# A decoder layer in one kernel: half-pace solve, merged columns turned outside TensorE, and the output projection's first steps

## The chip, the cores and the metric

The kernel runs on one core of one Trainium2 chip. The metric is the device time of one execution in microseconds. In the texts PE is TensorE (with PEld its weight loads), DVE is VectorE, ACT is ScalarE, POOL is GpSimd and SP is SyncE, whose queue issues nearly all transfers here.

## The reference

One decoder layer on 256 tokens of width 2048, all in fp32. The parts that bear on the change:

```python
def rms_norm(x, w):
    xf = x.astype(jnp.float32)
    y = xf * lax.rsqrt(jnp.mean(xf * xf, axis=-1, keepdims=True) + NORM_EPS)
    return (y * w.astype(jnp.float32)).astype(x.dtype)

# in chunk_gated_delta_rule, per head and chunk
t_mat = lax.linalg.triangular_solve(eye + a_mat, jnp.broadcast_to(eye, a_mat.shape),
                                    left_side=True, lower=True, unit_diagonal=True)
u = jnp.einsum('bhncs,bhnsv->bhncv', t_mat, v * beta[..., None])
...
```

The layer computes h = rms_norm(x) and projects it. Two branches follow, a gated delta rule of 8 heads (branch A, which holds the triangular solve above) and block-sparse attention of 8 heads (branch B). Each branch is taken to width 2048 by a matrix of its own, both are multiplied by sigmoid gates that are projected from h, and they are added ("merged"). An output projection of the merged values is added to x. A second norm and a gated MLP of width 5632, with a convolution of width 3, end the layer, and a last norm gives the output.

## The kernel before

Every product of width is done as three products of fp32r halves: a weight chunk of 128x2048 is fetched by SP into one of four buffers `wraw` (`fetch`, L121), cast by ACT in two pieces to `wh` (L111), and DVE writes the rest `wl` = raw - `wh` (L108). `wh` and `wl` have two buffers each, so ACT can cast a chunk only when PE has finished the chunk before the last. One chunk gives PE 24 matmuls with 512 moving columns, or as many columns in pairs of 512 and 256.

The work beside the weights runs as generators in the list `bg`. `main_mm` (L100 to 105) adds up the columns of the weight matmuls and calls `tick` after every 8 matmuls of 512 columns, and a tick advances each generator to its next `yield`. All engines take their instructions in program order, so the ticks set where this work stands between the weight matmuls on PE, the casts on ACT and the `wl` subtractions on DVE.

The stages around the change, in order:

- **Branch A's solve** (`gdn_unit`, L534 to 654) is done twice, for heads 0 to 3 (unit 0) and 4 to 7 (unit 1). The 32x32 diagonal blocks are inverted by 31 steps of two DVE instructions each (L561 to 567), a transfer to DRAM and back (tiles `dT` and `TL`, L568 and L570) puts them in place, and after 12 ticks DVE transposes 32x32 blocks (L574, tile `U`). Two levels of small matmuls with PE, DVE and POOL in turn, then `u`, `r`, `u`, `po` follow, each a tick apart. After `po`, POOL squares (L635), DVE reduces (L637), ACT takes a root, DVE scales (L644, tile `ot`), and four ticks later PE transposes 8 blocks (`pot`, L652). Unit 1 runs beside the gate projections:

```python
            if r % (2 - u["n"]) == 0:
                yield
```

so unit 0 does two steps a tick and unit 1 one.

- **Gates** (L756 to 769): 8 groups of 512 columns, `by_token`, in tiles `gts`. Before the sigmoids of group 4, unit 1 must have ended:

```python
        if c == 4:
            while ("end", 1) not in done:
                tick()
```

- **Branch projections** (L800 to 810): for each group c of 512 columns, 2 chunks of `w_ba` and 2 of `w_bb`, PSUM tiles `ps_br` with tokens on partitions. DVE multiplies by the gates and adds (L804 to 809). `merged(c, i)` (L789 to 798) then has PE transpose four 128x128 blocks of the 128 tokens i (`pt_m`, L794), ACT copies the result to `mc` and DVE writes the low half. `mc` has channels on partitions.
- **Output projection** (L819 to 843): 8 column groups `ps_wo` of two chunks each. The PSUM pools are opened anew (L812). The first group starts before the last merged group is there, by `steps`, and L160 lets the remaining ticks run before the step `flush`.
- **rstd** (L214 to 221) sums squares over the partitions by fp32 matmuls with a matrix of ones: two for the first norm (R1), four for the second (R2).
- **Down projection** (L875 to 911): the eight PSUM banks are taken in a fixed order.

Of the kernel before, what the change touches and what calls it, by code (L numbers as in the profile page):

```python
# [11 lines left out]
F32 = mybir.dt.float32  # L12
# [3 lines left out]
ALU = mybir.AluOpType  # L16
AX = mybir.AxisListType
PSUM = bass.MemoryType.PSUM

P = 128  # L20
# [53 lines left out]
def layer_kernel(ctx: ExitStack, tc: tile.TileContext, xT, pos, cst, ceye, vec, convw, ffw, bdv,  # L74
# [72 lines left out]
    def psum_pools(mm, sd):  # L147
        if pst[2]:
            pst[2].close()
        pst[2] = ExitStack()  # L150
        pst[0] = pst[2].enter_context(tc.tile_pool(name="ps_mm", bufs=mm, space=PSUM, reuse_waits="tile"))
        pst[1] = pst[2].enter_context(tc.tile_pool(name="ps_sd", bufs=sd, space=PSUM, reuse_waits="tile"))

    psum_pools(3, 5)

# [59 lines left out]
    def rstd(parts, tp, name):  # L215
        ps = sdt(name)[:, :T]
        mmg(ps, [(ones, t) for t in parts])
        r = tp.tile([P, T], F32, name=name)
        act.activation(r, ps, AF.Sqrt, bias=epst, scale=1.0 / D)
        dve.reciprocal(r, r)  # L220
        return r
# [67 lines left out]
        dve.tensor_tensor(sq[2], sq[2], sq[3], op=ALU.add)  # L289
    dve.tensor_tensor(sq[0], sq[0], sq[2], op=ALU.add)  # L290
    dve.tensor_tensor(sq[0][:, 0:2], sq[0][:, 0:2], sq[0][:, 2:4], op=ALU.add)


    wb2 = g.tile([P, KD, 48], F32R, name="wb2")
# [2 lines left out]
    low(wb2[:, :, 0:16], wb2[:, :, 32:48], wbd)  # L297
    s = sdt("ps_bd")[:48, :T]
    mmg(s, [(wb2[:, k, :], x_[:, k, :]) for k in range(KD) for x_ in (hh, hl)])
    R1 = rstd([sq[0][:, 0, :], sq[0][:, 1, :]], fk, "R1")  # L300
    R1b = both(R1)
    beta = fk.tile([16, T], F32, name="beta")
    sint = fk.tile([48, T], F32, name="sint")
# [235 lines left out]
    def gdn_unit(u):  # L539
# [21 lines left out]
        for r in range(30, -1, -1):  # L561
            tm = gu.tile([P, 8, 32], F32, name="tm", tag="Tm", bufs=1)
            n = 32 - r
            dve.tensor_tensor(tm[:, :, :n], X[:, :, r:], N[:, r:r + 1, r:].to_broadcast([P, 8, n]), op=ALU.mult)
            dve.tensor_reduce(X[:, :, r], tm[:, :, :n], axis=AX.X, op=ALU.add, negate=True)
            if r % (2 - u["n"]) == 0:
                yield
        pool.dma_start(bass.AP(tensor=dT.tensor, offset=dT.offset, ap=[[32 * P + 32, 32], [8 * P, 4], [P, 8], [1, 32]]), X)  # L568
        TL = gu.tile([P, 8, P], F32, name="TL", tag="u", bufs=1)
# [86 lines left out]
    def pair(w, i):  # L656
        return [w[2 * i], w[2 * i + 1]]
# [128 lines left out]
    m = m_st.enter_context(tc.tile_pool(name="mp", bufs=1, reuse_waits="tile"))  # L786
    mc = m.tile([P, KD * 2 * T + 128], F32R, name="mc")[:, SHIFT:SHIFT + KD * 2 * T].rearrange("p (k a t) -> p k a t", a=2, t=T)

    def merged(c, i):  # L789
        g_ = gts[0][:, i, c, :]  # L790
        yield
        pt = sdt("pt_m")
        for j in range(4):
            pe.transpose(pt[:, j * P:(j + 1) * P], g_[:, j * P:(j + 1) * P], identm)  # L794
        d = mc[:, 4 * c:4 * c + 4, :, i * P:(i + 1) * P]
        with tc.high_priority():
            act.copy(d[:, :, 0, :], r3(pt, P))
            dve.tensor_tensor(d[:, :, 1, :], r3(pt, P), d[:, :, 0, :].bitcast(F32), op=ALU.subtract)

    for c in range(4):  # L800
        ps = by_token(w_ba[2 * c:2 * c + 2], yc[0], H, "ps_br")
        for i in range(2):
            with tc.high_priority():
                dve.tensor_tensor(gts[0][:, i, c, :], ps[i], gts[0][:, i, c, :], op=ALU.mult)  # L804
        ps = by_token(w_bb[2 * c:2 * c + 2], yc[1], H, "ps_br")
        for i in range(2):
            with tc.high_priority():
                dve.tensor_tensor(gts[1][:, i, c, :], ps[i], gts[1][:, i, c, :], op=ALU.mult)
                dve.tensor_tensor(gts[0][:, i, c, :], gts[0][:, i, c, :], gts[1][:, i, c, :], op=ALU.add)
            bg.append(merged(c, i))  # L810
    wide[0] = True
    psum_pools(3, 2)  # L812

# [4 lines left out]
    h2 = hp.tile([P, KD, 2, T], F32R, name="h2", tag="hc")  # L818
    for c in range(8):  # L819
        if c == 0:  # L820
            steps = ((0, 0, KD - 4), (1, 0, KD - 4), (0, KD - 4, KD), (1, KD - 4, KD))
            ps = chunk(pair(w_o, c), mc, KD, "wo", steps=steps, flush=2)
            y_st.close()
            bkeep = bk.enter_context(tc.tile_pool(name="bkeep", bufs=1, side="right", reuse_waits="tile"))
            x1 = bkeep.tile([P, KD, T], F32, name="x1")
            ffv = bkeep.tile([P, 88, 4], F32, name="ffv")
            sp.dma_start(ffv, ffw)
        else:
            ps = chunk(pair(w_o, c), mc, KD, "wo")
        if c % 2 == 0:  # L830
            s = slice(2 * c, 2 * c + 4)
            sp.dma_start(x1[:, s, :], xT[:, s, :])
        xc = x1[:, 2 * c:2 * c + 2, :]
        for a in (1, 0):
            dve.tensor_tensor(xc, xc, ps[:, :, a, :], op=ALU.add)
        scaled(xc, ln2v, 2 * c, h2[:, :, 0, :], h2[:, :, 1, :])
        if c == 0:
            act.activation(sqa, xc, AF.Square)
        else:
            sq = b.tile([P, 2, T], F32, name="sq2")  # L840
            act.activation(sq, xc, AF.Square)
            if c < 7:
                pool.tensor_tensor(sqa, sqa, sq, op=ALU.add)
    R2 = rstd([t[:, j, :] for t in (sqa, sq) for j in range(2)], bkeep, "R2")
    R2b = both(R2)
    bp.close()
    m_st.close()
# [24 lines left out]

    ps_d = ctx.enter_context(tc.tile_pool(name="ps_d", bufs=1, space=PSUM, reuse_waits="tile"))
    pd = [[ps_d.tile([P, 512], F32, name=f"pd{i}_{n}") for n in range(4)] for i in range(2)]
    order = [(1, 2), (1, 3), (0, 2), (0, 3), (1, 0), (1, 1), (0, 0), (0, 1)]  # L875

    def residual(i, n):
        for j in range(4):
# [118 lines left out]
```

## Time and profile before

| | us |
|---|---|
| median of 3 runs | 1494.66 |
| runs, lowest and highest | 1494.28, 1494.69 |
| the profiled execution | 1494.29 |
| its span | 1492.5 |
| PE busy | 1473.2 (99% of the span) |
| DVE, ACT, POOL busy | 989.9, 728.8, 177.2 |
| PE's share of the chain that ended last | 98% |

The page gives busy time by engine, the chain of work that ended last, and the costliest groups of instructions. The chain is followed back from the last instruction, at each step to what released it. Where PE has 98% of it, the rest is to be read at the few places at which the chain leaves PE. The views of the trace used below are the waits by engine, the chain of a stretch, windows with busy time and granted clock, timelines of one engine, and the groups of transfers.

### The profile page before, as it was taken

To read this page: it belongs to the slowest core of one execution; us is meant where nothing else is said; L and a number is where in the kernel's file an instruction comes from. 1 tells how busy PE (TensorE), PEld (TensorE's weight loads), DVE (VectorE), ACT (ScalarE), POOL (GpSimd) and SP (SyncE) were. 2 spreads that over 40 slices of the span, in tenths; PEclk is the share of its full clock that TensorE was granted. 3 is DMA by queue.
4 is the path that set the end of the run, shared out by engine and by line. 5 is a ranking of instruction groups with operands and counts; after the bars stand their busy time and mean duration, and the time that the engine had idled before them with its cause. 6 is when DMAs were issued, how large, how long until landed. Compare 5 with 4: busy or idle time off the path is not lost.

```text
span 1492.5 us, 20716 instructions
## 1 busy us (share of the span) xinstructions
PE 1473.2 (99%) x8383; PEld 1296.7 (87%) x8383; DVE 989.9 (66%) x1397; ACT 728.8 (49%) x969; POOL 177.2 (12%) x135
## 2 busy tenths in 40 slices
PE   9999999999999799999999999999999999999997
PEld 8898899999888688888888888888888888888886
DVE  6997866888844445657766776766767766555554
ACT  5665445554443544435455555555545554444444
POOL 0112000433000400000101111121121110000000
PEclk9999999999999899999999999999999999999999
DMA  9455553544654255556555555555555554555552
GB/s 343 171 189 197 201 184 114 173 159 167 210 194 149 85 210 187 195 210 218 179 218 186 187 192 197 187 184 195 197 175 195 196 187 179 189 190 189 196 196 85
DMA packets 44432, 278.14 MB, mean 186 GB/s; under 512 B 5560, under 2 KB 7664, under 8 KB 12208
## 3 DMA queue, kind: packets, MB, share of 16 engines
q1 hardware_dynamic: 41456, 270.98, 50.7%
q0 software_dynamic: 2016, 3.68, 0.8%
q10 hardware_dynamic: 864, 2.16, 0.4%
q8 instruction: 65, 1.06, 0.3%
q14 instruction: 31, 0.25, 0.0%
HBM read 273.65 MB, written 3.15 MB: 185 GB/s over the span
## 4 chain that ended last, share of the span: by engine, by line
PE 98%; ACT 0%; DMA 0%; DVE 0%; POOL 0%; issue 0%; SPq 0%; DVEq 0%; ACTq 0%; POOLq 0%
PE ps_up L101 33%; PE pd L89 16%; PE ps_gate L101 12%; PE ps_gdn L101 8%; PE ps_moba L101 6%; PE ps_wo L101 6%; PE ps_br L101 6%; PE ps_z L101 3%; PE ps_v L101 3%; PE ps_gdn L257 1%; PE g L89 1%; PE pu L604 0%; PE py L598 0%; DMA xs<-in_xT 0%; PE ps_bd L89 0%; PE po L89 0%
## 5 line engine op out<-in xcount | busy, mean ns | idle before, releaser
L108 DVE TENSOR_TENSOR wl<-wraw,wh 128x1024 fp32r<-128x1024 f32 x496 | 601.3, 1249 | 256.8 <-ACT wh L111 256.6
L111 ACT CAST wh<-wraw 128x1024 fp32r<-128x1024 f32 x496 | 495.3, 1046 | 390.3 <-PE ps_up L101 117.3
L101 PE MATMUL ps_up<-h,wh 128*128 128x512 f32 x1408 | 488.6, 390 | 0.0
L101 PE MATMUL ps_up<-h,wl 128*128 128x256 f32 x1408 | 397.0, 282 | 0.0
L101 PEld LDWEIGHTS ps_up<-h,wh 128*128 128x128 f32 x1408 | 264.2, 188 | 55.4
L101 PEld LDWEIGHTS ps_up<-h,wl 128*128 128x128 f32 x1408 | 266.1, 189 | 0.1
L101 PE MATMUL ps_gate<-wh,hc 128*128 128x512 f32 x512 | 158.4, 395 | 2.8 <-ACT gts L769 2.8
L865 POOL TENSOR_TENSOR acts<-sg,cvf 128x256 f32<-128x256 f32 x44 | 80.8, 1837 | 423.3 <-ACT sg L864 423.3
L89 PE MATMUL pd<-wl,ah 128*128 128x512 f32 x336 | 130.8, 389 | 0.0
L89 PE MATMUL pd<-wh,al 128*128 128x512 f32 x336 | 130.8, 389 | 0.0
L101 PE MATMUL ps_gdn<-hc,wh 128*128 128x256 f32 x704 | 127.1, 281 | 0.0
L101 PEld LDWEIGHTS ps_gate<-wh,hc 128*128 128x128 f32 x512 | 96.7, 190 | 22.9 <-ACT gts L769 3.2
L101 PEld LDWEIGHTS ps_gdn<-hc,wh 128*128 128x128 f32 x704 | 108.3, 188 | 0.4
L859 ACT ACTIVATE cvf<-unf,ffv 128x256 f32<-128x256 f32 x88 | 48.2, 595 | 104.5 <-DVE unf L207 104.5
L101 PE MATMUL ps_gate<-wl,hc 128*128 128x512 f32 x256 | 98.9, 395 | 0.0
L861 DVE SCALAR_TENSOR_TENSOR cvf<-unf,ffv,cvf 128x254 f32<-128x254 f32 (+1 forms) x176 | 77.3, 481 | 32.1 <-ACT cvf L859 31.8
L101 PE MATMUL ps_gdn<-hc,wl 128*128 128x256 f32 x352 | 98.4, 280 | 0.0
L101 PE MATMUL ps_moba<-hc,wh 128*128 128x256 f32 x512 | 92.2, 281 | 0.0
L101 PE MATMUL ps_wo<-mc,wh 128*128 128x512 f32 x256 | 89.0, 390 | 0.4 <-ACT wh L111 0.4
L89 PE MATMUL pd<-wh,ah 128*128 128x512 f32 x336 | 86.7, 391 | 0.0
L111 ACT CAST ah<-acts 128x256 fp32r<-128x256 f32 x44 | 17.9, 406 | 126.0 <-PE pd L89 116.3
L101 PEld LDWEIGHTS ps_moba<-hc,wh 128*128 128x128 f32 x512 | 78.7, 188 | 0.0
(423 smaller groups left out, 1861.6 us busy)
## 6 DMA issues: line engine op xcount, KB each, us to landing
wraw<-in_w_up SPq DMA_DIRECT2D x88, 1024.0 KB, 4.8
wraw<-in_w_dn SPq DMA_DIRECT2D x44, 1024.0 KB, 4.8
wraw<-in_w_gate SPq DMA_DIRECT2D x32, 1024.0 KB, 4.8
wraw<-in_w_gdn SPq DMA_DIRECT2D x22, 1024.0 KB, 4.8
wraw<-in_w_moba SPq DMA_DIRECT2D x16, 1024.0 KB, 4.8
wraw<-in_w_o SPq DMA_DIRECT2D x16, 1024.0 KB, 4.8
wraw<-in_w_z SPq DMA_DIRECT2D x8, 1024.0 KB, 5.4
wraw<-in_w_mv SPq DMA_DIRECT2D x8, 1024.0 KB, 4.8
```

Source lines behind the costliest of these rows:

```text
L89: pe.matmul(ps, a, b, start=(start and i == 0), stop=(stop and i == n - 1), **kw)
L101: pe.matmul(ps, a, b, start=start, stop=stop, skip_group_check=True)
L108: return (eng or dve).tensor_tensor(lo, src, hi.bitcast(F32), op=ALU.subtract)
L111: act.copy(hi, src)
L257: pe.matmul(ps_q0[:, b], r3(wq[b], P)[:, k], xs[:, k], start=(k == b == 0), stop=(k == KD - 1), skip_group_check=True)
L859: act.activation(t[:, j, :], un[:, j, :], AF.Identity, scale=w[:, 2:3], bias=w[:, 3:4])
L861: dve.scalar_tensor_tensor(t[:, j, d:], un[:, j, :T - d], w[:, 2 - d:3 - d], t[:, j, d:], op0=ALU.mult, op1=ALU.add)
L865: pool.tensor_tensor(acts[:, c, :], sg, t[:, 1, :], op=ALU.mult)
```

## The change

Five edits.

1. `r % 2` for both units: unit 1's solve takes 16 ticks instead of 31, two steps in each.
2. The merged groups c = 0, 1, 2 are no longer transposed on PE. `moved(c)` has DVE transpose 32x32 blocks of two 128x512 tiles into a buffer, 16 transfers of 32x8x32 on SP's queue put the blocks where a full transpose has them, in a second buffer, and ACT and DVE write `mc` from there. The buffers (`turned`) have the tag of `hc`, whose last readers are the gate projections, and `h2` has it after them. Group 3 goes through PE as before.
3. The output projection's first group goes by other steps (two chunks, the first finished three quarters of the way before the second begins), the remaining ticks run before its second step, and the PSUM pool of the small tiles is opened ahead of the wide one, which puts the wide tiles on other banks.
4. One more DVE addition for R1 and one more POOL addition for R2 leave one and three matmuls of ones.
5. The bank order of the down projection is changed.

```diff
--- before.py
+++ after.py
@@ -148,8 +148,9 @@
         if pst[2]:
             pst[2].close()
         pst[2] = ExitStack()
-        pst[0] = pst[2].enter_context(tc.tile_pool(name="ps_mm", bufs=mm, space=PSUM, reuse_waits="tile"))
-        pst[1] = pst[2].enter_context(tc.tile_pool(name="ps_sd", bufs=sd, space=PSUM, reuse_waits="tile"))
+        for i in ((0, 1), (1, 0))[wide[0]]:
+            pst[i] = pst[2].enter_context(tc.tile_pool(name=("ps_mm", "ps_sd")[i], bufs=(mm, sd)[i], space=PSUM,
+                                                       reuse_waits="tile"))
 
     psum_pools(3, 5)
 
@@ -289,6 +290,7 @@
         dve.tensor_tensor(sq[2], sq[2], sq[3], op=ALU.add)
     dve.tensor_tensor(sq[0], sq[0], sq[2], op=ALU.add)
     dve.tensor_tensor(sq[0][:, 0:2], sq[0][:, 0:2], sq[0][:, 2:4], op=ALU.add)
+    dve.tensor_tensor(sq[0][:, 0], sq[0][:, 0], sq[0][:, 1], op=ALU.add)
 
 
     wb2 = g.tile([P, KD, 48], F32R, name="wb2")
@@ -297,7 +299,7 @@
     low(wb2[:, :, 0:16], wb2[:, :, 32:48], wbd)
     s = sdt("ps_bd")[:48, :T]
     mmg(s, [(wb2[:, k, :], x_[:, k, :]) for k in range(KD) for x_ in (hh, hl)])
-    R1 = rstd([sq[0][:, 0, :], sq[0][:, 1, :]], fk, "R1")
+    R1 = rstd([sq[0][:, 0, :]], fk, "R1")
     R1b = both(R1)
     beta = fk.tile([16, T], F32, name="beta")
     sint = fk.tile([48, T], F32, name="sint")
@@ -563,7 +565,7 @@
             n = 32 - r
             dve.tensor_tensor(tm[:, :, :n], X[:, :, r:], N[:, r:r + 1, r:].to_broadcast([P, 8, n]), op=ALU.mult)
             dve.tensor_reduce(X[:, :, r], tm[:, :, :n], axis=AX.X, op=ALU.add, negate=True)
-            if r % (2 - u["n"]) == 0:
+            if r % 2 == 0:
                 yield
         pool.dma_start(bass.AP(tensor=dT.tensor, offset=dT.offset, ap=[[32 * P + 32, 32], [8 * P, 4], [P, 8], [1, 32]]), X)
         TL = gu.tile([P, 8, P], F32, name="TL", tag="u", bufs=1)
@@ -786,6 +788,27 @@
     m = m_st.enter_context(tc.tile_pool(name="mp", bufs=1, reuse_waits="tile"))
     mc = m.tile([P, KD * 2 * T + 128], F32R, name="mc")[:, SHIFT:SHIFT + KD * 2 * T].rearrange("p (k a t) -> p k a t", a=2, t=T)
 
+
+    turned = hp.tile([P, 3, 2, 8, P], F32, name="turned", tag="hc")
+
+    def moved(c):
+        a_, b_ = turned[:, c, 0], turned[:, c, 1]
+        for i in range(2):
+            dve.transpose(a_[:, 4 * i:4 * i + 4, :].rearrange("p k t -> p (k t)"), gts[0][:, i, c, :])
+        yield
+        for a in range(4):
+            for e in range(4):
+                sp.dma_start(b_[32 * e:32 * e + 32, :, 32 * a:32 * a + 32], a_[32 * a:32 * a + 32, :, 32 * e:32 * e + 32])
+            yield
+        yield
+        yield
+        for i in range(2):
+            d = mc[:, 4 * c:4 * c + 4, :, i * P:(i + 1) * P]
+            v_ = b_[:, 4 * i:4 * i + 4, :]
+            act.copy(d[:, :, 0, :], v_)
+            dve.tensor_tensor(d[:, :, 1, :], v_, d[:, :, 0, :].bitcast(F32), op=ALU.subtract)
+            yield
+
     def merged(c, i):
         g_ = gts[0][:, i, c, :]
         yield
@@ -807,7 +830,10 @@
             with tc.high_priority():
                 dve.tensor_tensor(gts[1][:, i, c, :], ps[i], gts[1][:, i, c, :], op=ALU.mult)
                 dve.tensor_tensor(gts[0][:, i, c, :], gts[0][:, i, c, :], gts[1][:, i, c, :], op=ALU.add)
-            bg.append(merged(c, i))
+            if c == 3:
+                bg.append(merged(c, i))
+        if c < 3:
+            bg.append(moved(c))
     wide[0] = True
     psum_pools(3, 2)
 
@@ -818,8 +844,8 @@
     h2 = hp.tile([P, KD, 2, T], F32R, name="h2", tag="hc")
     for c in range(8):
         if c == 0:
-            steps = ((0, 0, KD - 4), (1, 0, KD - 4), (0, KD - 4, KD), (1, KD - 4, KD))
-            ps = chunk(pair(w_o, c), mc, KD, "wo", steps=steps, flush=2)
+            steps = ((0, 0, 8), (0, 8, 12), (1, 0, 4), (0, 12, KD), (1, 4, KD))
+            ps = chunk(pair(w_o, c), mc, KD, "wo", steps=steps, flush=1)
             y_st.close()
             bkeep = bk.enter_context(tc.tile_pool(name="bkeep", bufs=1, side="right", reuse_waits="tile"))
             x1 = bkeep.tile([P, KD, T], F32, name="x1")
@@ -841,7 +867,9 @@
             act.activation(sq, xc, AF.Square)
             if c < 7:
                 pool.tensor_tensor(sqa, sqa, sq, op=ALU.add)
-    R2 = rstd([t[:, j, :] for t in (sqa, sq) for j in range(2)], bkeep, "R2")
+            if c == 6:
+                pool.tensor_tensor(sqa[:, 0], sqa[:, 0], sqa[:, 1], op=ALU.add)
+    R2 = rstd([sqa[:, 0, :], sq[:, 0, :], sq[:, 1, :]], bkeep, "R2")
     R2b = both(R2)
     bp.close()
     m_st.close()
@@ -872,7 +900,7 @@
 
     ps_d = ctx.enter_context(tc.tile_pool(name="ps_d", bufs=1, space=PSUM, reuse_waits="tile"))
     pd = [[ps_d.tile([P, 512], F32, name=f"pd{i}_{n}") for n in range(4)] for i in range(2)]
-    order = [(1, 2), (1, 3), (0, 2), (0, 3), (1, 0), (1, 1), (0, 0), (0, 1)]
+    order = [(0, 0), (0, 1), (1, 0), (1, 1), (1, 2), (1, 3), (0, 2), (0, 3)]
 
     def residual(i, n):
         for j in range(4):
```

PE around the end of unit 1, the gate projections before: `u`, `po` and `pot` are unit 1's last matmuls, and the rows `ps_gate` are weight matmuls.

```order
L101 MATMUL ps_gate<-wh,hc 128x512 x2
L101 MATMUL ps_gate<-wl,hc 128x512
L621 MATMUL u_4652<-vb,U 128x128 x4
L628 MATMUL po<-x,aq 128x128 x4
L89 MATMUL po<-x,aq 128x128 x8
L652 MATMUL pot<-ct,ot 128x128 x8
L101 MATMUL ps_gate<-wh,hc 128x512 x2
L101 MATMUL ps_gate<-wl,hc 128x512
```

In the changed kernel, the same engine, at the first `po`:

```order
L101 MATMUL ps_gate<-wl,hc 128x512
L101 MATMUL ps_gate<-wh,hc 128x512
L623 MATMUL u_4488<-vb,U 128x128 x4
L630 MATMUL po<-x,aq 128x128 x4
L89 MATMUL po<-x,aq 128x128
L101 MATMUL ps_gate<-wh,hc 128x512
```

and, 65 matmuls of the gates later, at `pot`:

```order
L101 MATMUL ps_gate<-wh,hc 128x512 x2
L101 MATMUL ps_gate<-wl,hc 128x512
L654 MATMUL pot<-ct,ot 128x128
L101 MATMUL ps_gate<-wh,hc 128x512 x2
L654 MATMUL pot<-ct,ot 128x128 x4
L101 MATMUL ps_gate<-wl,hc 128x512
L654 MATMUL pot<-ct,ot 128x128 x3
L101 MATMUL ps_gate<-wh,hc 128x512 x2
```

The small matmuls that stood in one run of 24 now stand in pieces between weight matmuls.

SP's queue from the branch projections to the output projection, before (`wraw` are weight chunks, `x` is the residual input):

```order
L121 DMA wraw<-in_w_ba 128x2048 x2
L121 DMA wraw<-in_w_bb 128x2048 x2
L121 DMA wraw<-in_w_ba 128x2048 x2
L121 DMA wraw<-in_w_bb 128x2048 x2
L121 DMA wraw<-in_w_o 128x2048 x6
L827 DMA ffv<-in_ffw 128x352
L832 DMA x_5922<-in_xT 128x1024 x4
```

and now:

```order
L121 DMA wraw<-in_w_ba 128x2048 x2
L121 DMA wraw<-in_w_bb 128x2048 x2
L121 DMA wraw<-in_w_ba 128x2048 x2
L801 DMA turned<-turned 32x8x32 x16
L121 DMA wraw<-in_w_bb 128x2048 x2
L121 DMA wraw<-in_w_ba 128x2048 x2
L801 DMA turned<-turned 32x8x32 x16
L121 DMA wraw<-in_w_bb 128x2048 x2
L121 DMA wraw<-in_w_o 128x2048 x2
L801 DMA turned<-turned 32x8x32 x16
L121 DMA wraw<-in_w_o 128x2048 x4
```

Each group of 16 transfers stands ahead of a weight fetch that it did not stand ahead of before.

ACT through the branch projections, before (`wh` are casts of weight pieces, `mc` the copies of merged groups, `gts` the last gate):

```order
L769 ACTIVATE gts<-ps_gate,cols 128x512
L111 CAST wh<-wraw 128x1024 x8
L797 CAST mc<-pt_m 128x4x128 x2
L111 CAST wh<-wraw 128x1024 x8
L797 CAST mc<-pt_m 128x4x128 x2
L111 CAST wh<-wraw 128x1024 x8
```

and now:

```order
L771 ACTIVATE gts<-ps_gate,cols 128x512
L111 CAST wh<-wraw 128x1024 x14
L808 CAST mc<-turned 128x4x128 x2
L111 CAST wh<-wraw 128x1024 x8
L808 CAST mc<-turned 128x4x128 x2
L111 CAST wh<-wraw 128x1024 x8
L808 CAST mc<-turned 128x4x128 x2
L111 CAST wh<-wraw 128x1024 x2
```

The copies of group 0 come 6 casts later than they did, those of groups 1 and 2 keep 8 casts between them, and those of group 3 stand 2 casts behind group 2's.

## Rows read from the trace of the kernel before

**Rows 1.** Page, section 1: busy time, share of the span, instructions.

```profile
PE 1473.2 (99%) x8383; PEld 1296.7 (87%) x8383; DVE 989.9 (66%) x1397; ACT 728.8 (49%) x969; POOL 177.2 (12%) x135
```

**Rows 2.** Waits of PE: total us, times, longest us.

```profile
PE pot L652 <- DVE ot L644: 5.2, 1, 5.2
PE ps_gate L101 <- ACT gts L769: 2.8, 1, 2.8
```

**Rows 3.** Chain of waits, 495 to 508 us: start, length, what.

```profile
495.61 1.80 PE po L89 x16
...
498.16 1.90 POOL so L635
...
500.08 1.23 DVE st L637
...
505.71 1.28 ACT L769
...
507.74 1.65 PE ps_gate L101 x3
```

**Rows 4.** Windows: PE, PEld, DVE, ACT, POOL busy (instructions), granted clock, DMA share, GB/s.

```profile
506.00:509.00 3.00, 1.26 (x3) 1.06 (x4) 0.00 (x0) 2.99 (x5) 0.14 (x1) 0.50 0.00 0
509.00:512.00 3.00, 3.00 (x8) 2.32 (x8) 0.00 (x0) 3.00 (x7) 3.00 (x3) 0.50 0.00 0
570.00:660.00 90.00, 90.00 (x411) 74.52 (x410) 56.73 (x61) 35.93 (x40) 0.00 (x0) 1.00 0.52 188
660.00:674.00 14.00, 12.90 (x76) 11.02 (x75) 6.71 (x9) 5.68 (x8) 0.00 (x0) 1.00 0.75 291
```

**Rows 5.** Timeline of DVE, 398 to 450 us: start, busy, what [idle before].

```profile
401.90 0.42 DVE L565 TENSOR_REDUCE X<-tm 128x8 f32<-128x256 f32 x1
...
413.75 2.36 DVE L108 TENSOR_TENSOR wl<-wraw,wh 128x1024 fp32r<-128x1024 f32 x2 [3.08 <-ACT wh L111]
...
444.25 1.24 DVE L574 STREAM_TRANSPOSE U<-TL 128x1024 f32<-128x1024 f32 x1
```

**Rows 6.** Tile TL: issues; duration ns, first and last start.

```profile
L570 POOL DMA_DIRECT2D TL<-dT x2: 897/900/902, 188.3 to 405.9; - x2
```

**Rows 7.** DMA issues: count, KB each, median us to landing.

```profile
wraw<-in_w_ba SPq DMA_DIRECT2D x8, 1024.0 KB, 4.8
...
TL<-dT POOLq DMA_DIRECT2D x2, 512.0 KB, 5.8
...
dN<-aq POOLq DMA_DIRECT2D x32, 8.0 KB, 2.6
...
dT<-X POOLq DMA_DIRECT2D x2, 128.0 KB, 3.6
```

**Rows 8.** Chain of waits around two transposed groups.

```profile
595.58 0.44 PE pt_m L794 x4
...
618.28 0.44 PE pt_m L794 x4
```

**Rows 9.** Timeline of SP, 575 to 700 us: start of first, time to last.

```profile
589.56 6.24 SPq L121 DMA_DIRECT2D wraw<-in_w_ba  x2
...
634.98 28.95 SPq L121 DMA_DIRECT2D wraw<-in_w_o  x6
...
665.86 1.85 SPq L832 DMA_DIRECT2D x<-in_xT  x4
```

**Rows 10.** Timeline of ACT, 608 to 616 us.

```profile
608.79 2.00 ACT L111 CAST wh<-wraw 128x1024 fp32r<-128x1024 f32 x2 [3.44 <-PE ps_br L101]
614.23 2.00 ACT L111 CAST wh<-wraw 128x1024 fp32r<-128x1024 f32 x2 [3.44 <-PE ps_br L101]
```

**Rows 11.** Timeline of DVE where the output projection begins.

```profile
659.88 0.69 DVE L808 TENSOR_TENSOR gts<-ps_br,gts 128x512 f32<-128x512 f32 x1 [0.62 <-PE ps_br L101]
```

**Rows 12.** Chain of waits, 745 to 760 us: the second norm's sum.

```profile
751.10 0.86 PE R L89 x4
```

**Rows 13.** Timeline of POOL, 738 to 760 us.

```profile
743.41 1.48 POOL L843 TENSOR_TENSOR sqa<-sqa,sq 128x512 f32<-128x512 f32 x1 [9.61 <-ACT sq L841]
```

## The prediction

> **What bounds the kernel.** I read the page's busy times first. PE is busy for 1473.2 of 1492.5 us, DVE for 989.9 and ACT for 728.8 [rows 1]. So a time can only come from work taken off PE or from PE's 19.3 us of idle time, and a loss only from a new PE wait. Next I read PE's waits: the longest inside the kernel is one of 5.2 us for `ot` and one of 2.8 us for a gate [rows 2]. The chain of that stretch shows why: `po` ends at 497.41 (495.61 + 1.80), then POOL, DVE and ACT work one after another, PE has only the `pot` transposes, and an ACT table load of 1.28 us stands before the sigmoid that PE waits for. Weight matmuls resume at 507.74 [rows 3]. The windows then give the granted clock: 0.50 of full from 506 to 512, that is the lower of the two levels, 1.2 GHz, after PE had been mostly idle, and 1.00 over 570 to 660, where PE is busy without a gap [rows 4].
>
> **Part 1, the half-pace solve.** Unit 1's 31 steps end at 402.32 (401.90 + 0.42) and its next DVE instruction, the transpose of U, comes at 444.25, after 16 weight splits [rows 5]. By the program it stood there because 31 yields and 12 more ticks lay ahead of it; now it is 16 and 12. Fifteen ticks of 8 matmuls are 5 weight chunks of 24, and a chunk is 5.44 us (608.79 to 614.23 [rows 10]): 27.2 us. U's transpose now stands after 6 splits, by the old times at 416.1 (413.75 + 2.36 [rows 5]). Its input was issued at 405.9 [rows 6] and lands 5.8 us later [rows 7], at 411.7: 4.4 us to spare, so no wait takes the place of the ticks. Everything of unit 1 behind it comes 27 us earlier too, and then `po` and `pot` stand between weight matmuls, 65 of them (14.7 us at 5.44/24 = 0.227 each) between the first `po` and `pot`. The chain from `po` to `ot` took 497.41 to 502.44, 5.0 us [rows 2, 3]: covered nearly three times. What goes away: 507.74 − 497.41 = 10.33 us, less the 8 `pot` transposes that remain (two groups of four like `pt_m`, 0.44 each [rows 8]), is 9.45. Then from 507.74 to 512 PE did 4.26 us of work at clock 0.50 [rows 4], of which half, 2.13, was lost. Together **−11.6 us**. What is tight afterwards: ACT must do two `ya` copies, a table load and two sigmoids between `pot` and the next gate group, and then the eight casts of `yc`, which all stood in that stretch before. By their times in the trace the weight casts behind them come within about half a microsecond of PE's need. I put 0 to 1 us there, and take 0.4.
>
> **Part 2, three groups off PE.** A group's four transposes are 0.44 us in the chain. From the first group of c = 0 to that of c = 1 it is 22.70 us (595.58 to 618.28 [rows 8]), and 4 chunks of 5.44 are 21.76, so two transposed groups cost 0.94, or 0.47 each with what they interrupt. Six go: 2.64 to 2.82, **−2.7 us**. In their place stand six DVE transposes of 128x512. The nearest row is the 128x1024 one of 1.24 us [rows 5], so some 0.62 each, 3.7 in all, on a DVE that is busy 56.7 of 90 us there [rows 4]: hidden. ACT's and DVE's copies to `mc` only change their source.
>
> The unknown is the 48 transfers, each 32 KB in 256 runs of 128 bytes. SP issues about one each 0.46 us (four in 1.85 us [rows 9]), 7.4 us for a group. By the program the eighth of a group waits for the landing of the weight fetch before it, since eight counters serve the queue, and the last eight each wait for one of the first eight. For c = 0 the fetch is issued at 595.5 (the second of the pair begun at 589.56 [rows 9]) and lands 4.8 later [rows 7], so the issue ends near 604.4 (600.3 + 9 × 0.46). How long one takes to land has no row of its own. From below, `dN<-aq` of 64 such runs lands in 2.6 us; from above, `dT<-X` of 1024 runs lands in 3.6 [rows 7], and a whole group has four times its runs, so 4 × 3.6 = 14.4 if nothing overlaps. The group is thus there between 607 (604.4 + 2.6) and 614.7 (600.3 + 14.4). I take 608, near the first, because a single one is nearer to 64 runs and they overlap in their queue. ACT's copies stand after the pair of casts that ends at 610.79, and the next cast began at 614.23 [rows 10]. That cast was ready 1.06 later and PE needs it one chunk later, at 619.67, so with both copies (0.6 each) and DVE's work behind them about 616 is still harmless. Even the upper bound fits. For c = 2 the fetch is the second `w_o`, near 640.8 (634.98 + 28.95/5 [rows 9]), so it lands at 645.6 and the group between 652.3 and 660.0; ACT reaches these copies two periods of 22.70 after 610.79, at 656.2: 4 us to spare, or 4 us late by the upper bound. The fetch behind each group is issued some 3 us later than before, and it is used about four chunks after its issue. `h2`, which takes the buffer of the blocks, is first written behind the last of these copies in ACT's own order. **Cost 0**, from 0 to 5 us.
>
> The Trainium skill speaks against these transfers: "DMA: Bandwidth & Descriptors", Rules for kernel authors, says to coalesce small transfers, which are mostly overhead under 64 KB, and its section on the anatomy of one DMA gives about 2.0 us fixed for each. An estimate from that page's figure, if they ran one after another, is 32 us a group; the trace's 2.6 us for a small one agrees with a fixed part of that size, but no run here shows whether 16 of them overlap.
>
> **Part 3, the output projection's entry.** From 660 to 674 PE is busy 12.90 us of 14 [rows 4]: 1.10 idle. The first part waits for the bank of the last gate product, which DVE multiplies from 659.88 to 660.57 [rows 11], and the rest for the first column's next weights, whose buffer came free only after the third of the four steps. Now the wide tile begins on banks that DVE left one product earlier, and the first column ends 12 row blocks before the second begins, 4.2 us for a cast and a split that take 1.06 + 1.24. DVE's additions there are behind one more split, so some of it can stay: **−0.8**, from 0 to −1.1.
>
> **Part 4, the sums of squares.** Four records of `R` are 0.86 us, and one fp32 matmul is two of them, so 0.43 [rows 12]. One of two goes at R1 and one of four at R2, two in all, **−0.86**. The POOL addition that replaces the second is half of one of 1.48 us that began at 743.41 [rows 13], and done near 745.6, over 5 us before R2 at 751.10. DVE's is as early at R1. Part 5 only follows the banks: 0.
>
> **The sum.** 1494.29 − 11.6 − 2.7 − 0.8 − 0.9 + 0.4 = 1478.7 against the profiled execution. The median of the runs is 0.4 above that execution, so 1479.1; I say **1479**.
>
> **The rivals.**
> - *The drain is only partly gone.* ACT has `st`'s root, two table loads and the casts in one order; a root that waits for POOL and DVE holds the weight casts behind it, and the casts of `yc` come in one block. For it speaks that ACT had the same block at 505 to 512 [rows 3, 4]; against it, that PE has 14.7 us of matmuls for a chain of 5.0. If half of part 1's 11.6, or somewhat less or more, comes back that way, it is 1482 to 1487.
> - *Transfers somewhat late.* The upper bound holds, c = 2 is 4 us late, and the fetches behind are pushed: 1482 to 1487.
> - *Transfers one after another, slower than before.* At 2.6 us each [rows 7] a group takes 42 us and lands near 638 instead of 608. ACT takes its instructions in order, so the casts wait behind the copies, and PE runs out 22 us past the harmless 616. Three groups are +65, less 15.6 won: about 1544. It decides from 1.3 us a transfer, (616 − 596)/16. Against it: the program lets eight be in flight, and a fetch of 1 MB lands in 4.8 us [rows 7], so the queue moves far more than 32 KB at once. By the 2.0 us of the Trainium skill ("DMA: Bandwidth & Descriptors", the anatomy of one DMA) a group would land at 628, 12 us late each time, and the estimate would be about 1515.
> - *The drain stays.* If U's data came late, or the loop for the end of unit 1 still met a late tick, part 1 would give nothing: 1490 to 1491.
>
> **How the numbers follow.** Forecast (1475.5 to 1482) 0.63; drain partly there 0.14; transfers somewhat late 0.11; drain stays 0.05; one after another 0.07. The low end takes no new stalls and all of part 3, and some of the remaining idle; the two middle rivals set the high end, 1488; what is left out is 0.05 + 0.07 and a little of the rest. A measurement of this kernel can tell about 0.2%, 3 us, from no change. Faster is the first three and a part of "drain stays", whose 1490 to 1491 lies just under the bound of 1491.7, 0.90; same is the rest of that, 0.03; slower is the transfers one after another, 0.07.
>
> **What would show it.** PE's wait for `ot` and that for the gate at group 4 gone, clock 1.00 there, `pot` between gate matmuls; U's transpose near 416; two `pt_m` groups left instead of eight; the transfers landing within 3 us of their issue and no idle time of PE before `ps_br`; the gap at 660 to 674 under 0.4 us; three `R` matmuls at R2. A PE wait on a weight cast whose ACT idled before `mc` would prove the transfers slow.

## The result and the profile after

The changed kernel takes 1477.68 us in the median of 4 runs (1477.59 to 1477.95). The kernel before, on the same chip, takes 1494.47 (1493.91 to 1494.69). The ratio is 0.9888, with a 95% interval of 0.9871 to 0.9906, so 16.8 us are gone. The profiled execution of the changed kernel took 1477.95 us with a span of 1476.2, which is 16.3 shorter than before.

The page's line of busy times, which answers to [rows 1], shows PE busy 7.8 us less, and its idle time down from 19.3 to 10.8 us:

```profile
PE 1465.4 (99%) x8355; PEld 1291.1 (87%) x8355; DVE 994.2 (67%) x1404; ACT 728.3 (49%) x969; POOL 177.4 (12%) x136
```

The 7.8 us are not all work taken off PE, for a matmul that runs slowly is busy longer. Windows over the whole gate stage, before and after (columns as in [rows 4]), have the same 920 instructions on PE with 8.0 us less idle time and 3.8 us less busy time:

```profile
365.70:569.80 204.10, 196.06 (x920) 163.55 (x920) 109.10 (x148) 89.29 (x111) 22.20 (x15) 0.97 0.47 166
...
365.40:557.70 192.30, 192.30 (x920) 161.20 (x919) 109.90 (x148) 88.52 (x111) 22.26 (x15) 1.00 0.49 176
```

In the changed kernel PE waits like this (total us, times, longest us). The waits for `ot` and for the gate of [rows 2] are gone, and those that are left are the start of the kernel and 0.2 us at the output projection:

```profile
PE ps_gdn L258 <- DMA xs<-in_xT: 1.2, 1, 1.2
...
PE ps_wo L101 <- DVE mc L821: 0.2, 1, 0.2
```

Most can be read from where each stage's first matmul starts, in the two traces:

| stage, from the first start of its tile to that of the next | before | after | difference |
|---|---|---|---|
| gates (`ps_gate` to `ps_br`) | 365.7 to 569.8: 204.1 | 365.4 to 557.7: 192.3 | −11.8 |
| branch projections (`ps_br` to `ps_wo`) | 569.8 to 660.7: 90.9 | 557.7 to 644.7: 87.0 | −3.9 |
| output projection (`ps_wo` to `ps_up`) | 660.7 to 751.6: 90.9 | 644.7 to 735.1: 90.4 | −0.5 |
| up projection (`ps_up` to `pd`) | 751.6 to 1240.8: 489.2 | 735.1 to 1224.3: 489.2 | 0.0 |

The branch and output projections are best read together, as −4.4: one of the two transposed groups of c = 3, some 0.4 us, stood ahead of the first `ps_wo` matmul before (659.68) and stands behind it now (647.53).

**The solve.** On DVE's timeline, where [rows 5] had U's transpose at 444.25, it now starts at 415.68, right behind the sixth split. No wait stands ahead of it:

```profile
413.40 2.36 DVE L108 TENSOR_TENSOR wl<-wraw,wh 128x1024 fp32r<-128x1024 f32 x2 [3.08 <-ACT wh L111]
415.68 1.23 DVE L576 STREAM_TRANSPOSE U<-TL 128x1024 f32<-128x1024 f32 x1
```

In the chain of waits (start, length, what), the small matmuls that ran as one block in [rows 3] stand between weight matmuls. From the end of the first `po` rows (474.51) to `pot` (490.87) PE never stops:

```profile
473.39 0.89 PE po L630 x8
474.29 0.22 PE po L89 x2
474.51 3.65 PE ps_gate L101 x16
478.16 1.56 PE po L89 x14
479.72 11.14 PE ps_gate L101 x49
490.87 0.11 PE pot L654
```

ACT's timeline behind `pot` has the table load and the sigmoids as [rows 3] had them. The sigmoids end at 497.27, and PE went on without a wait:

```profile
493.43 1.26 ACT L655 ACTIVATE ya<-pot,vc 128x512 f32<-128x512 f32 x2
494.71 1.28 ACT L771 ACT_TABLE_LOAD   x1
496.00 1.27 ACT L771 ACTIVATE gts<-ps_gate,cols 128x512 f32<-128x512 f32 x2
```

The windows (PE, PEld, DVE, ACT and POOL busy, granted clock, DMA share, GB/s) show the clock at 1.00 all through that stretch, where [rows 4] had 0.50 for six microseconds, and 0.23 us of idle time at the entry of the output projection instead of 1.10:

```profile
463.00:505.00 42.00, 42.00 (x210) 35.32 (x209) 19.43 (x25) 25.40 (x34) 9.03 (x6) 1.00 0.42 151
645.00:660.00 15.00, 14.77 (x88) 12.87 (x87) 10.02 (x13) 7.56 (x10) 0.00 (x0) 1.00 0.93 353
```

**The transfers.** SP's timeline (first start, time to the end of the last) has three groups of 16, which take 10.6 to 11.6 us to issue:

```profile
584.17 10.55 SPq L801 DMA_DIRECT2D turned<-turned  x16
...
606.44 11.56 SPq L801 DMA_DIRECT2D turned<-turned  x16
...
628.20 10.55 SPq L801 DMA_DIRECT2D turned<-turned  x16
```

The view of the tile `turned` gives the durations of an issue and of a DVE transpose in ns (least, median, most), and the time to landing:

```profile
L801 SPq DMA_DIRECT2D turned<-turned x48: 585/608/1485, 584.2 to 638.1; - x48
...
L797 DVE STREAM_TRANSPOSE turned<-gts x6: 700/702/711, 579.1 to 627.5; 128x512 f32<-128x512 f32 x6
...
DMA to landing us min/median/max: 1.9/2.0/5.3
```

The landing times are of two kinds. The first seven transfers of group 0 were issued while the weight fetch ahead of them was still under way, and landed only behind it; the other nine took 2.0 us (DMA issues from 583.4 to 588.9 and from 588.9 to 594.5: count, KB each, median us to landing):

```profile
wraw<-in_w_ba SPq DMA_DIRECT2D x1, 1024.0 KB, 5.4
turned<-turned SPq DMA_DIRECT2D x7, 32.0 KB, 3.7
...
turned<-turned SPq DMA_DIRECT2D x9, 32.0 KB, 2.0
```

Groups 1 and 2 show the same (medians of 4.4 and 3.9 us for the first seven). The last transfer of a group landed 11.9, 12.9 and 13.2 us after the group's first issue.

ACT's timeline shows when the copies to `mc` came. Group 0's data were there when ACT reached the copies at 597.65, and the next cast still found PE not ready (2.39 us idle). For group 2 ACT waited 0.26 us for a landing:

```profile
597.65 1.14 ACT L808 CAST mc<-turned 128x512 fp32r<-128x512 f32 x2
...
601.19 2.00 ACT L111 CAST wh<-wraw 128x1024 fp32r<-128x1024 f32 x2 [2.39 <-PE ps_br L101]
...
641.54 1.15 ACT L808 CAST mc<-turned 128x512 fp32r<-128x512 f32 x2 [0.26 <-DMA turned<-turned]
```

**Entry and sums.** In the chain at the output projection's entry PE now waits for the copy and the low half of the last merged group, 1.4 us on the chain, of which 0.2 is idle:

```profile
649.76 0.45 PE pt_m L817 x4
...
650.23 0.59 ACT mc L820
...
650.85 0.70 DVE mc L821
...
651.59 28.58 PE ps_wo L101 x163
```

The second norm's sum: the first row is POOL's sum, with two records where [rows 12] had four; the second is the two matmuls for the last squares, which are in both kernels.

```profile
735.07 0.43 PE R L89 x2
...
740.35 0.86 PE R L89 x4
```

### The profile page after: what moved, and what is told of

It reads as the page before. It is cut to its first block, busy times and chain, and to the rows that moved or that the text cites. A ratio compares the mean times of both kernels' runs of the same rounds, so it can differ in the third digit from the quotient of the medians.

```text
span 1476.2 us, 20730 instructions
## 1 busy us (share of the span) xinstructions
PE 1465.4 (99%) x8355; PEld 1291.1 (87%) x8355; DVE 994.2 (67%) x1404; ACT 728.3 (49%) x969; POOL 177.4 (12%) x136
## 4 chain that ended last, share of the span: by engine, by line
PE 99%; DMA 0%; DVE 0%; SPq 0%; ACT 0%; issue 0%; DVEq 0%; ACTq 0%
PE ps_up L101 33%; PE pd L89 16%; PE ps_gate L101 12%; PE ps_gdn L101 8%; PE ps_moba L101 6%; PE ps_wo L101 6%; PE ps_br L101 6%; PE ps_z L101 3%; PE ps_v L101 3%; PE ps_gdn L258 1%; PE g L89 1%; PE pu L606 0%; PE py L600 0%; DMA xs<-in_xT 0%; PE ps_bd L89 0%; PE po L89 0%
## 5 line engine op out<-in xcount | busy, mean ns | idle before, releaser
L101 PEld LDWEIGHTS ps_gate<-wh,hc 128*128 128x128 f32 x512 | 95.7, 188 | 19.5
L89 PE MATMUL pd<-wh,ah 128*128 128x512 f32 x336 | 92.8, 391 | 0.0
```

The lines of the kernel that those rows point to most:

```text
L89: pe.matmul(ps, a, b, start=(start and i == 0), stop=(stop and i == n - 1), **kw)
L101: pe.matmul(ps, a, b, start=start, stop=stop, skip_group_check=True)
```

## The experiments

Each run is compared with runs of the kernel before on its own chip; their medians agree within 0.2 us from chip to chip, so the times are also set against the changed kernel's 1477.68. Where a stage is named, it is between the starts given in the table above, taken in that run's own trace. The stages agree from trace to trace better than the total times, because the wait for the first input at the start of the kernel alone varied from 0.3 to 1.9 us.

**Only the solve's pace, on the kernel before.**

```diff
-            if r % (2 - u["n"]) == 0:
+            if r % 2 == 0:
```

> The kernel before with only the solve's pace changed (two steps a tick in both units). Theory: part 1 is worth 11.6 us by itself, the drain's idle time, its slow pot transposes and the half-clock matmuls, so 1494.5 - 11.6 = 1482.9, between 1482.3 and 1483.6; PE's waits for ot and for the gate at group 4 are gone and the granted clock stays at 1.00. Rival (drain partly there): a root, the table loads or the casts of yc hold weight casts and 1484 to 1487 comes out.

Measured: 1483.66 us (1482.09 to 1484.06) against 1494.56, ratio 0.9923 (0.9911 to 0.9936), 10.9 us. The gate stage went from 365.7 to 558.0, 192.3 us, exactly as in the changed kernel: −11.8, and its span of 1480.7 is 11.8 below 1492.5. The total times scatter by 2 to 3 us on that chip, and their median lies 0.1 us above the expected range. Windows of this run at the place of [rows 4]:

```profile
506.00:509.00 3.00, 3.00 (x15) 2.49 (x14) 3.00 (x3) 0.00 (x0) 3.00 (x2) 1.00 0.41 109
509.00:512.00 3.00, 3.00 (x14) 2.47 (x14) 3.00 (x2) 2.00 (x2) 3.00 (x2) 1.00 0.58 243
```

PE is full and the clock is at 1.00, and PE's waits for `ot` and for the gate are gone. The theory holds by itself, without the other edits.

**The transposes back on PE.** In the changed kernel, `bg.append(merged(c, i))` for all four groups.

```diff
-            if c == 3:
-                bg.append(merged(c, i))
-        if c < 3:
-            bg.append(moved(c))
+            bg.append(merged(c, i))
```

> The changed kernel with all four merged groups transposed on TensorE again, no blocks turned by DVE and no transfers of them. Theory: six groups of four transposes come back at 0.44 to 0.47 us each and the transfers cost nothing, so 1477.7 + 2.6 to 2.8 = 1480.4. Rival (transfers somewhat late cost part of what they save): 1478 to 1479.5.

Measured: 1480.09 us (1479.79 to 1480.53), 2.4 above the changed kernel; `ps_br` to `ps_up` is 179.8 against 177.4, also 2.4. The transposes are worth what they take, less the 0.2 us wait for `mc`, which this run does not have.

**The moved groups alone, on the kernel before.** The function `moved`, the buffer and the condition above put into the kernel before.

> The kernel before with only the three merged groups moved off TensorE (blocks turned by DVE, 48 transfers on SP's queue). Theory: 2.6 to 2.8 us of transposes go and the entry of the output projection loses up to 0.5 by DVE's additions behind a split, so 1494.5 - 2.2 = 1492.3, between 1491.6 and 1492.6, with the drain's waits for ot and the gate unchanged. Rival: on its own it loses the gain again at the entry, 1494.

Measured: 1492.06 us (1491.44 to 1492.49, 11 runs) against 1494.65, ratio 0.9982 (0.9973 to 0.9990). `ps_br` to `ps_up` is 179.2 against 181.8: −2.6. The waits of 5.2 and 2.8 us in the drain (the stretch at the end of unit 1, [rows 3]) are there unchanged. With this and the run before, 2.4 to 2.6 us is shown from both sides.

**The old entry of the output projection.**

```diff
-            steps = ((0, 0, 8), (0, 8, 12), (1, 0, 4), (0, 12, KD), (1, 4, KD))
-            ps = chunk(pair(w_o, c), mc, KD, "wo", steps=steps, flush=1)
+            steps = ((0, 0, KD - 4), (1, 0, KD - 4), (0, KD - 4, KD), (1, KD - 4, KD))
+            ps = chunk(pair(w_o, c), mc, KD, "wo", steps=steps, flush=2)
```

with the old order of the pools and of the down projection's banks.

> The changed kernel with the output projection's steps, flush and PSUM pool order of before, and the bank order of the down projection that goes with them. Theory: the 1.1 us of idle time at the entry comes back where the changed kernel has 0.2, so +0.9, 1478.6, between 1478.0 and 1479.2. Rival: the entry was only late because of the transposes beside it, and nothing comes back, 1477.7.

Measured: 1479.74 us (1478.72 to 1481.38), above the expected range, and `ps_br` to `ps_up` 178.7, 1.3 more than the changed kernel (the total times are 2.1 above and scatter by 2.7). PE's waits in this run:

```profile
PE ps_wo L101 <- DVE wl L108: 0.7, 1, 0.7
PE pt_m L817 <- DVE gts L832: 0.5, 1, 0.5
```

The wait for `wl` is the old one. The wait of `pt_m` for a gate product (DVE's addition at L832) is new: with the moved groups DVE has that addition behind one more split, and the run with the moved groups alone has the same wait of 0.5. So the new entry is worth 1.3 us beside the moved groups, more than the 0.9 that came from the old trace alone; the two waits, less the changed kernel's 0.2, are 1.0 of it. The steps, the flush and the pool order were not tested one by one.

**The old sums of squares**: two matmuls of ones for R1 and four for R2.

> The changed kernel with the sums of squares of before: two matmuls of ones for R1 and four for R2. Theory: two fp32 matmuls of 0.43 us come back in full, 1477.7 + 0.86 = 1478.5. Rival: at R1 or R2 PE had a gap beside them, +0.43 or less.

Measured: 1478.48 us (1478.24 to 1478.90), +0.8. The two matmuls are on the path in full.

**A solve of 24 ticks.** The expectation counts 23, but the condition gives 24: the 16 even steps and 8 more.

```diff
-            if r % 2 == 0:
+            if r % 2 == 0 or (u["n"] and r % 4 == 1):
```

> The changed kernel with unit 1's solve spread over 23 ticks instead of 16, 7 ticks (12.7 us) later. po then still stands between gate matmuls, 39 of them ahead of pot, but the eight pot transposes stand together behind group 4's last matmul, as the drain had them. Theory: the wait for ot is nearly covered, only the wait for the sigmoids (two ya copies, a table load, a sigmoid) of 2.8 us comes back, so 1480.5 to 1481.2, without a fall of the granted clock. Rival: whatever ends in the drain costs all of it, 11.6, so 1489.

Measured: 1484.12 us (1483.64 to 1485.40), +6.4, and the gate stage is 198.3 us, +6.0. U's transpose came at 432.73, 17.1 us later than in the changed kernel. PE's waits:

```profile
PE ps_gate L101 <- ACT gts L771: 2.8, 1, 2.8
...
PE pot L654 <- DVE ot L646: 0.7, 2, 0.4
```

The two waits are as the theory said, 2.8 and 0.7. But PE went from the end of its last gate matmul at 497.25 to the next at 502.54. In these 5.29 us it had the two waits and the eight `pot` transposes, which took 1.85 us here and take 0.88 between weight matmuls (8 at 0.11), so 4.4 are lost. And then the granted clock was low:

```profile
500.00:503.00 3.00, 0.46 (x1) 0.46 (x2) 0.00 (x0) 2.97 (x5) 0.00 (x0) 0.84 0.00 0
503.00:506.00 3.00, 3.00 (x9) 2.33 (x9) 0.00 (x0) 3.00 (x7) 2.34 (x2) 0.59 0.00 0
506.00:509.00 3.00, 3.00 (x14) 2.45 (x14) 0.81 (x1) 3.00 (x5) 3.00 (x4) 1.00 0.00 0
```

Matmuls ran at half the clock until about 505.3, 2.8 us, of which 1.4 are lost: 4.4 + 1.4 = 5.8 of the 6.0 measured. The theory had the waits and missed the clock; the rival, all 11.6 back, fell as well. It shows how the drain's 11.8 us divide: 6.0 come with `pot` and the sigmoids standing together, and 5.8 with `po` and its chain standing there too.

**24 transfers a group.** The same bytes, half of the 16 transfers cut in two.

```diff
-                sp.dma_start(b_[32 * e:32 * e + 32, :, 32 * a:32 * a + 32], a_[32 * a:32 * a + 32, :, 32 * e:32 * e + 32])
+                for k in ((0, 4), (4, 8)) if e < 2 else ((0, 8),):
+                    sp.dma_start(b_[32 * e:32 * e + 32, k[0]:k[1], 32 * a:32 * a + 32],
+                                 a_[32 * a:32 * a + 32, k[0]:k[1], 32 * e:32 * e + 32])
```

> The changed kernel with half of the 16 transfers of a group cut in two, 24 a group, the same bytes; ACT's order is the same. A group then lands about 5 us later. Theory (ACT takes its copies in order, with about 3.4 us of slack before a cast is late): groups 0 and 1 cost nothing, group 2 makes the output projection wait 2 to 4 us, so 1479.5 to 1481.5. Rival by the prediction's point of 1.3 us a transfer (a group of 21 us is still harmless): 1477.7.

Measured: 1482.59 us (1481.90 to 1482.77), +4.9 and 1.1 above the expected range, and `ps_br` to `ps_up` 182.1, +4.7. ACT's timeline, with its waits for group 1, for group 2 and for a weight fetch:

```profile
622.79 1.15 ACT L810 CAST mc<-turned 128x512 fp32r<-128x512 f32 x2 [2.96 <-DMA turned<-turned]
...
647.58 1.14 ACT L810 CAST mc<-turned 128x512 fp32r<-128x512 f32 x2 [5.98 <-DMA turned<-turned]
...
651.83 2.00 ACT L111 CAST wh<-wraw 128x1024 fp32r<-128x1024 f32 x2 [3.11 <-DMA wraw<-in_w_o]
```

Group 2's issue on SP is below. The planner, which sets the order of each engine's instructions, had also put one fetch that stands ahead of each group in the changed kernel behind it:

```profile
626.58 19.51 SPq L802 DMA_DIRECT2D turned<-turned  x24
```

PE's waits:

```profile
PE pt_m L819 <- DVE gts L834: 2.2, 1, 2.2
```

Groups 0 and 1 were harmless, group 1 although ACT waited 2.96 us. Group 2 cost all of it, by two ways that both begin with the longer issue: the copies held DVE's low halves, and with them the gate addition that `pt_m` needs (2.2 us), and the next weight chunk came late (ACT idle 3.11 for a fetch), and with it the last copies (PE waited 0.7 for `mc`, where the changed kernel has 0.2); after the first of these pauses the granted clock was 0.72 for six microseconds (650 to 656). Over 641 to 660 us PE idled 2.9 us, 0.2 of which the changed kernel has too, and 0.28 of six is 1.7 more: 4.4 of the 4.7. The rival, 21 us a group harmless, fell.

**The transfers done twice, the second after the first.**

```diff
-                sp.dma_start(b_[32 * e:32 * e + 32, :, 32 * a:32 * a + 32], a_[32 * a:32 * a + 32, :, 32 * e:32 * e + 32])
+                for _ in range(2):
+                    sp.dma_start(b_[32 * e:32 * e + 32, :, 32 * a:32 * a + 32],
+                                 a_[32 * a:32 * a + 32, :, 32 * e:32 * e + 32])
```

> The changed kernel with each of the 48 transfers done twice over, the second waiting for the first, so that a group takes 16 landings one after another; the planner puts ACT's copies of group 0 six casts later. Theory (the rival of the prediction): at 2.6 us a group takes 42 us, ACT holds the casts behind the copies and SP's queue holds the weight fetches, and 1515 to 1545 comes out, with PE's waits at weight casts. Other: eight landings overlap even so and it is under 1490.

Measured: 1511.79 us (1510.49 to 1512.11), ratio to before 1.0113 (1.0098 to 1.0128): slower than before. It came out a little under the expected range, and not for the reason given. SP's timeline:

```profile
584.34 21.75 SPq L802 DMA_DIRECT2D turned<-turned  x31
...
607.42 24.13 SPq L802 DMA_DIRECT2D turned<-turned  x32
```

The first two groups took 22 to 24 us each, not 42: the planner set several first transfers ahead of their seconds, so the landings of 2.0 us still overlapped, and the run does not show transfers one after another. And ACT's copies found their data (no wait ahead of them at 616.55); what ACT waited for was weights:

```profile
616.55 1.14 ACT L810 CAST mc<-turned 128x512 fp32r<-128x512 f32 x2
...
637.61 1.99 ACT L111 CAST wh<-wraw 128x1024 fp32r<-128x1024 f32 x2 [19.92 <-DMA wraw<-in_w_ba]
```

PE's waits for the casts behind those fetches are the largest entry:

```profile
PE ps_br L101 <- ACT wh L111: 26.8, 4, 14.4
```

So transfers that hold SP's queue cost through the fetches queued behind them. That ACT held the casts behind the copies is not what happened here, where group 0's copies stood six casts later.

**The transfers on POOL's queue**: `pool.dma_start` in place of `sp.dma_start`.

> The changed kernel with the 48 transfers issued from POOL's queue instead of SP's. The weight fetches then stand where they stood before. Theory (the transfers and the later fetches are both hidden): no change, 1477.3 to 1478.2. Rival (the fetches held up behind the blocks cost something now): faster by up to 0.5 us. Other: POOL's issue is slower than 0.6 us each and group 2 is late, 1479 to 1482.

Measured: 1478.96 us (1478.54 to 1480.38), +1.3, and `ps_br` to `ps_up` 178.6, +1.2. That is above the theory's range and at the edge of the third case's, though not by a slower issue. An issue takes about as long as on SP, but the median landing took over twice as long:

```profile
L801 POOL DMA_DIRECT2D turned<-turned x48: 582/582/617, 584.4 to 639.3; - x48
...
DMA to landing us min/median/max: 1.9/4.4/6.4
```

This is not shown to come from POOL's queue. SP went on fetching here, and each of the 48 transfers was under way at the same time as a weight fetch. The transfers of SP's queue for which that holds have medians of 3.7 us in the changed kernel and 4.4 and 4.5 in the two runs before this one, and the shortest from POOL took 1.9.

PE waits at the entry:

```profile
PE ps_wo L101 <- DVE mc L809: 1.3, 1, 1.3
```

The planner set each group's copies two casts later than in the changed kernel, so that PE met group 2's before DVE had done with them. That wait, less the changed kernel's 0.2, is 1.1 of the 1.2 us. The fetches went undelayed, and no gain from it can be seen: in the changed kernel PE waits for no weights, so their delay is hidden.

**Fewer sums and a longer step.** A version meant to be faster than both.

```diff
-            steps = ((0, 0, 8), (0, 8, 12), (1, 0, 4), (0, 12, KD), (1, 4, KD))
+            steps = ((0, 0, 8), (0, 8, 12), (1, 0, 8), (0, 12, KD), (1, 8, KD))
...
-    R2 = rstd([sqa[:, 0, :], sq[:, 0, :], sq[:, 1, :]], bkeep, "R2")
+    dve.tensor_tensor(sq[:, 0], sq[:, 0], sq[:, 1], op=ALU.add)
+    R2 = rstd([sqa[:, 0, :], sq[:, 0, :]], bkeep, "R2")
```

> The changed kernel with the last two squares added on DVE, so that R2 takes two matmuls of ones instead of three, and with the second column's first step in the output projection lengthened from 4 to 8 row blocks. Theory: one fp32 matmul of 0.43 us and the 0.2 us wait for mc at the entry go, 1477.7 - 0.65 = 1477.05. Rival: the added DVE instruction makes R2 or the first up-projection tiles wait, 1477.7 or above.

Measured: 1476.81 us (1476.43 to 1478.24), ratio to before 0.9885 (0.9869 to 0.9900). The wait for `mc` is gone, and R2 is two matmuls (four records, 0.86 us) in the chain:

```profile
734.67 0.43 PE R L89 x2
...
743.31 0.43 PE R L89 x2
```

From the first `ps_br` to the first `pd` matmul it is 665.7 us where the changed kernel has 666.6. The stage shows the gain of 0.9; the total times, whose runs overlap at 1477.6 to 1478.2, only suggest it.

## Why the prediction was right

The forecast was 1479 and the time is 1477.7, inside the likeliest case's own range. By its steps:

- **Part 1, −11.6.** Measured −11.8 in the gate stage, by itself and with the rest. U's transpose was put at 416.1 and came at 415.68. The 0 to 1 us for a tight spot, taken as 0.4, did not come: the sigmoids ended at 497.27 and PE found them ready. Two readings on the way were too good. `po` came 21.3 us earlier (its second rows from 495.61 to 474.29) and not 27. And of the 14.7 us of gate matmuls only the 11.1 behind the last `po` rows cover the chain, which had itself grown: `ot` began 6.7 us after the end of `po` (479.72 to 486.43 on DVE's timeline), where the drain had 4.7. So it was covered, but not nearly three times. Against the profiled execution the forecast was 1478.7, and that took 1477.95: 0.4 of the 0.75 is that term and 0.2 this part's. The other 0.6 of the 1.3 is how the medians stand to the profiled executions.
- **Part 2, −2.7.** Measured −2.4 to −2.6, and the transfers cost nothing, as said. But the reason had errors in both directions. One transfer lands in 2.0 us where no fetch is under way, below the lower bound of 2.6; behind a fetch the first of a group took 5.1 to 5.3, which the sign "within 3 us of their issue" did not foresee. SP issues one each 0.65 us and not 0.46, so from the issue of the fetch ahead of group 0 to the end of the group's own issue it took 11.2 us (583.5 to 594.7), where 8.9 was worked out. The 4 us to spare at group 2 were not there: the group was there 13.9 us after the issue of its fetch and not 11.5, and ACT reached the copies after 13.7 and not 15.4, so it waited 0.26 us for the last landing. The cost of 0 was thus right with less room than was thought.
- **The coalescing rule.** The landing of 2.0 us agrees with the fixed part of about 2.0 us that the Trainium skill states ("DMA: Bandwidth & Descriptors", the section on the anatomy of one DMA), though the page gives it for transfers issued from POOL and these are SP's. The estimate of 32 us a group, for transfers one after another, did not come about: 16 of them were there 11.9 to 13.2 us after the first issue, because one is issued each 0.65 us and takes 2.0 to land, so they overlap.
- **Part 3, −0.8.** Idle time at the entry went from 1.10 to 0.23, −0.9; beside the moved groups the old entry costs 1.3 more than the new one.
- **Part 4, −0.86.** Measured 0.8 by undoing it.
- **The rival on the other side**, transfers one after another, did not come about in the changed kernel. In the runs with more transfers it had the right sign and the wrong mechanism. It priced ACT's copies and called a group harmless up to 1.3 us a transfer. With 24 transfers at 16 to 19.5 us a group, 4.7 us were lost, and at 22 to 24 us a group 33.6 (`ps_br` to `ps_up` 211.0 against 177.4). It left out that the weight fetches stand behind the transfers in SP's queue, and that DVE has a gate addition behind the low halves of `mc`.

What stays open: how near the changed kernel's 16 transfers are to the point where the fetches are late. 24 were past it, but there the planner had also moved a fetch at each group, and the two were not separated. The bank order of the down projection (edit 5) was not tested by itself; the times from the first `pd` matmul to the end differ by 0.2 us (251.7 before, 251.9 after).

## What to carry to other kernels

Where small dependent steps of several engines stand together ahead of a wait, look at what sets their place: here a tick count, and moving them 21 us earlier was worth more (11.8 us) than removing work (2.4 for the transposes, 0.8 for the sums). Price such a pause as its idle time plus the half-clock work behind it; the second was 2.1 of 11.6 us in the drain by the prediction's working, and 1.4 of 5.8 in the run with 24 ticks. And when work moves from the bound engine to a queue, cost it at every instruction behind it in that queue, since the lost time appears at the engine that needs the delayed fetch.

## What the runs showed of the hardware that was not expected

- A transfer of 32 KB in 256 runs of 128 bytes between two places of SBUF lands in 2.0 us from SP's queue where no weight fetch is under way, and one of 16 KB in 1.8 to 1.9.
- Issued while a 1 MB weight fetch ahead of it was under way, the same transfer took 2.2 to 5.3 us and landed behind the fetch, in all three groups of the changed kernel (the first seven of each 16). The median of 4.4 us from POOL was taken under such fetches throughout.
- Its issue occupies SP for 0.61 us and one follows another each 0.65 us; the input transfers of [rows 9] follow each 0.46.
- The granted clock fell after 5.29 us in which PE had only the eight `pot` transposes (0.84 over the three microseconds from 500, 0.59 over the next three, 1.00 after that), about half as long a pause as the 10.3 us of the drain.
